# Reciprocal root of x on GpSimd, lambda product a slot later, first value projection in program order

## The chip, the cores and the metric

One core of one Trainium2 chip. The metric is the device time of one execution in microseconds (us), lower is better; the number compared is the median of several runs. The engines are named as in the profile: PE is TensorE, DVE is VectorE, ACT is ScalarE, POOL is GpSimd, and SP (SyncE) issues the weight loads. Each engine works through its own list of instructions in order; an instruction whose input isn't ready holds up everything behind it on that engine.

## What is computed

One layer of a hybrid encoder: batch 1, 256 tokens with 16 learned meta tokens ahead of them (272 in all), width 2048, in fp32.

```
def rms_norm(x, g):
    y = x * lax.rsqrt(jnp.mean(x * x, axis=-1, keepdims=True) + EPS)
    return y * g

h = concat([meta_tokens, x], axis=1)                  # 272 x 2048
u = rms_norm(h, norm_mix)
aq, ak, av, mq, mk, mv, mo, mg = split(u @ w_in)      # 1024 1024 1024 512 512 1024 1024 16
lam = exp(sum(lambda_q1 * lambda_k1)) - exp(sum(lambda_q2 * lambda_k2)) + lam_init
attn = diff_attention(rope(aq), rope(ak), av, lam)    # 8 heads, rope on a quarter of each part
ml = mlstm(silu(conv(mq, mk)), mv, gates=mg) gated by sigmoid(mo)   # 4 heads, both directions
h = h + concat([attn, ml]) @ w_out
u = rms_norm(h, norm_ffn)
h = h + (silu(u @ w_gate) * (u @ w_up)) @ w_down
out = rms_norm(h, norm_final)[16:]
```

## The kernel before

**Products in two halves.** Each fp32 product is made of three matmuls: weights are split into a high half wh, cast on ACT (line 205, with the norm's gain as scale), and a low half wl, the difference, on DVE (line 206); the input is split the same way into uh and ul. For every 128 rows k of the contraction and each of four column tiles j, PE adds wh x uh, wh x ul and wl x uh into an accumulator in PSUM (lines 251 to 253). The reciprocal root of x's norm isn't multiplied into x. It is applied to the results later: to queries and keys through the rope tables, to values as a scale.

**Pieces.** A projection of 512 columns is eight pieces of 256 rows, 512 KB each, named aq0_0, ak0_3, av_2 and so on. SP issues their loads in order; four raw buffers and four pairs of wh and wl exist. PE works on two pieces at a time, tile by tile: 48 matmuls. Four accumulators (accp) hold the four column tiles, so the next projection starts with an accumulator when the last one's has been copied out: value_copy (line 614) by ACT, into vt_q, vt_k, vt_a. Two more banks (smp) serve small products such as prs, pc, plam, pgate, psi and pct.

**The order of projections** is aq, ak, av for the first four heads (g = 0, lines 941 to 959), the same for the other four, then those of the mLSTM, the output projection and the feed-forward part. The first one, aq, is written out by hand (lines 435 to 468): x is transposed on PE, split on ACT and DVE, and its squares are summed on ACT on the way. From the sums ssx the generator x_rstd (lines 333 to 344) makes the reciprocal root of the three mean squares per partition (two blocks of tokens and the meta tokens): a first guess by integer arithmetic on the bits, three Newton steps, all on a 128x3 corner of rs3, and then rmat, the result spread over 128 columns. Its instructions come out in rstd_steps, a few with each k from 10 on. In x_broadcast (lines 346 to 354) PE transposes rmat into prs after half of the last 48 matmuls of aq, and ACT copies it to rbc; the rope tables (cst) and the gates are scaled by rbc.

**Work beside the projections** comes from generators. slot() (line 174) advances each of them by one yield with every second piece. setup() (lines 484 to 498) transposes the small vectors into cols, multiplies the lambda vectors (lprod) on DVE, and sums the products on PE (plam). gates() (lines 547 to 607) makes the mLSTM's gate terms: pgate and psi on PE, logarithms on ACT, running sums and maxima by scans on DVE (gF, gx), then gn, gem and the halves gnh and gnl, and transposes of ga and gem on PE (pct). The ropes of the four heads (rope, line 812) are issued by a hook with pieces 1 to 4 of the next projection: a shuffle and a product on DVE, a product and a sum on POOL. attention() begins with stack(h) (line 832), which splits queries and keys of a head into halves qs, ks and klow.

**What sets the order on each engine.** A scheduler puts instructions in order by a simulated time and by priorities. Where code calls pin(...), which is keep_in_program_order (line 198), the instruction stays in the order of the program text among the pinned ones. In the kernel before, all of aq is pinned, the first piece of ak, and (pins=4) the three that follow it; the splits of av, the ropes of the heads, the gate steps and attention are not.

Of the kernel before, what the change touches and what calls it, by code (L numbers as in the profile page):

```python
# [86 lines left out]
def tile_hybrid_encoder_layer(  # L87
# [42 lines left out]
    def f(ap):  # L130
        return ap.bitcast(F32)
# [201 lines left out]
    def x_rstd():  # L333
        ms, y, t, h = (rs3[:, 3 * i:3 * i + 3] for i in range(4))
        yield V.tensor_reduce(ms[:, 0:2], ssx[:, :8].rearrange("p (b c) -> p b c", c=4), AX.X, ALU.add)
        yield V.tensor_copy(ms[:, 2:3], ssx[:, 8:9])
        yield V.tensor_scalar(ms, ms, 1.0 / D, EPS, ALU.mult, ALU.add)
        yield V.tensor_scalar(y.bitcast(I32), ms.bitcast(I32), -0.5, RSQRT_MAGIC, ALU.mult, ALU.add)
        yield V.tensor_scalar(h, ms, -0.5, None, ALU.mult)
        for _ in range(3):  # L340
            yield V.tensor_tensor(t, y, y, ALU.mult)
            yield V.tensor_tensor(t, t, h, ALU.mult)
            yield V.scalar_tensor_tensor(y, t, 1.5, y, ALU.add, ALU.mult)
        yield V.tensor_copy(rmat, rs3[:, 3:6, None].to_broadcast([P, 3, P]))

# [77 lines left out]
    def rstd_steps(n):  # L423
        for _ in range(n):
            ins = next(rstd, None)
            if ins is not None:
                pin(ins)
# [10 lines left out]
    for k in range(KD - TAILK):  # L438
# [4 lines left out]
        if k >= 10:  # L443
            rstd_steps(4 if k < 13 else 16)
        order = [(j, term) for j in range(4) for term in range(3)]
# [38 lines left out]
    def setup():  # L484
# [4 lines left out]
        lprod = mp.tile([64, 2], F32, name="lprod")  # L489
        V.tensor_tensor(lprod, cols[:64, V_LAM:V_LAM + 4:2], cols[:64, V_LAM + 1:V_LAM + 4:2], ALU.mult)  # L490
        yield
        plam = sm_tile("plam")
# [54 lines left out]
    def gates():  # L547
# [15 lines left out]
        def gt(name, w=NT):  # L563
# [23 lines left out]
        yield  # L587
        V.memset(gx, 0.0)
        V.tensor_tensor_scan(gx[:32], ones[:32], ga[:32], 0.0, ALU.mult, ALU.max)
        V.tensor_tensor_scan(  # L590
            gx[32:64, NM:][:, ::-1], ones[32:64, NM:], ga[32:64, NM:][:, ::-1], 0.0, ALU.mult, ALU.max
        )
        V.tensor_scalar(gn, gx[:, NM:], -1.0, None, ALU.mult)
        V.tensor_tensor(gem, gn, gF[:, NM:], ALU.subtract)
        A.copy(gnh[:64], apart(gn))
        V.tensor_tensor(gnl[:64], apart(gn), f(gnh[:64]), ALU.subtract)
        A.activation(gem, gem, AF.Exp)
        yield
        yield
# [211 lines left out]

    def rope(ps, t0, name):
        n = NT - t0
        dst = kpool.tile([P, n], F32, tag="qk", bufs=32, name=name)
        sh = mp.tile([P, NT], F32, tag="ev", bufs=4, name=f"sh_{name}")
        swap = list(range(8, 16)) + list(range(8)) + list(range(16, 32))
        V.stream_shuffle(sh[:, :n], ps[:, :n], swap)
        V.tensor_tensor(dst, ps[:, :n], ropeC[:, t0:], ALU.mult)
        G.tensor_tensor(sh[:, :n], sh[:, :n], ropeS[:, t0:], ALU.mult)
# [9 lines left out]
    def attention(h0, nh):  # L829
        es, at, hs, on, qs, ks = {}, {}, {}, {}, {}, {}  # L830

        def stack(h):
# [4 lines left out]
            for c in range(2):  # L837
# [4 lines left out]
                A.copy(ks[h][other, c], kc)  # L842
                V.scalar_tensor_tensor(
                    qs[h][other, c, :], q[own], QK_SCALE, f(qs[h][own, c, :]), ALU.mult, ALU.subtract
                )
                V.tensor_tensor(kz[own, c], kc, f(ks[h][own, c]), ALU.subtract)

# [85 lines left out]

    def roping(vts, t0, dst, name, g):
        def hook(i):
            if 1 <= i <= 4:
                dst[4 * g + i - 1] = rope(vts[i - 1], t0, f"{name}_{4 * g + i - 1}")

        return hook

    for g in range(2):
# [13 lines left out]
        vts = value_copy(accs, f"k{g}")  # L955
        accs = in_proj(C_AV + g * N_CHUNK, 0, f"av{g}", hook=roping(vts, 0, ak, "ak", g))
        vts = value_copy(accs, f"a{g}")
# [254 lines left out]
```

## Time and profile before

| | |
|---|---|
| median of 3 runs | 1129.65 us (1129.14 to 1129.94) |
| the profiled execution | 1129.36 us, span of the trace 1127.6 us |
| PE busy | 1112.6 us, 99% |
| DVE busy | 730.7 us, 65% |
| ACT busy | 655.5 us, 58% |
| POOL busy | 246.8 us, 22% |
| read from HBM | 209.45 MB, 188 GB/s over the span |

The span runs from the first to the last instruction in the trace; the device time is 1.8 us longer. Shares are averages over the whole span. A timeline row gives the start, the duration, engine, line, operation and tiles (output <- inputs); durations of neighbours can overlap, since an instruction starts while the one before it is still writing, so the distance from start to start is the step. "idle before <- releaser" is time in which the engine waited, and who ended it.

### The profile page before, as it was taken

How to read it: one execution, taken by the hardware profiler on the slowest of the kernel's cores; microseconds unless marked ns; L12 is line 12 of the kernel's file. 1: busy time of each engine (PE TensorE's matmuls, PEld its weight loads, DVE VectorE, ACT ScalarE, POOL GpSimd, SP SyncE). 2: the span in 40 equal slices, each digit the busy share in tenths (PEclk: the TensorE clock that was granted, in tenths of full speed). 3: DMA queues.
4: the chain of work that ended last, by engine and by line, in shares of the span. 5: the costliest groups of instructions: out<-in, count | busy, mean ns of one | idle time of the engine just before them, and what ended most of it. 6: DMA issues, size and time to landing. Idle time of an engine off the chain costs nothing.

```text
span 1127.6 us, 19817 instructions
## 1 busy us (share of the span) xinstructions
PE 1112.6 (99%) x7629; PEld 1040.6 (92%) x7629; DVE 730.7 (65%) x1121; ACT 655.5 (58%) x1199; POOL 246.8 (22%) x315
## 2 busy tenths in 40 slices
PE   8999999999999999999999999999999999999996
PEld 8889999999999999999999999999999888888896
DVE  6986987988875867556556655655655645444544
ACT  6568788789875545545545555554554644444443
POOL 7330230011045933222122122122122100000000
PEclk9999999999999999999999999999999999999998
DMA  8546545554545666576576666675666766666663
GB/s 267 173 139 198 150 151 165 153 169 144 157 150 175 190 200 199 176 229 188 189 229 190 190 222 188 197 221 188 199 222 185 244 207 202 199 196 205 194 199 112
DMA packets 112255, 212.85 MB, mean 189 GB/s; under 512 B 8906, under 2 KB 9744, under 8 KB 112016
## 3 DMA queue, kind: packets, MB, share of 16 engines
q1 hardware_dynamic: 111664, 210.48, 59.9%
q8 instruction: 60, 0.98, 0.4%
q10 hardware_dynamic: 176, 1.06, 0.3%
q14 instruction: 35, 0.29, 0.1%
q0 software_dynamic: 320, 0.04, 0.0%
HBM read 209.45 MB, written 2.10 MB: 188 GB/s over the span
## 4 chain that ended last, share of the span: by engine, by line
PE 92%; DVE 3%; DMA 1%; ACT 1%; issue 1%; POOL 1%; SPq 0%; ACTq 0%; DVEq 0%; POOLq 0%
PE acc_up L248 14%; PE acc_ga L248 14%; PE acc_ga L249 7%; PE acc_up L249 7%; PE acc_dn L1108 7%; PE acc_dn L1105 7%; PE acc_dn L1109 7%; PE acc_wo L253 2%; PE acc_wo L251 2%; PE acc_wo L252 2%; PE acc_mv L252 1%; PE acc_mv L251 1%; PE acc_mv L253 1%; PE acc_mo L252 1%; PE acc_mo L251 1%; PE acc_mo L253 1%
## 5 line engine op out<-in xcount | busy, mean ns | idle before, releaser
L248 PE MATMUL acc_ga<-vhl,wh_ga 128*128 128x512 f32 x704 | 227.4, 382 | 0.0
L248 PE MATMUL acc_up<-vhl,wh_up 128*128 128x512 f32 x704 | 227.0, 382 | 0.0
L213 DVE TENSOR_TENSOR wl_dn<-raw_dn,wh_dn 128x1024 fp32r<-128x1024 f32 x88 | 108.5, 1234 | 115.5 <-ACT wh_dn L212 115.5
L249 PE MATMUL acc_ga<-vhl,wl_ga 128*128 128x256 f32 x704 | 182.1, 273 | 0.0
L249 PE MATMUL acc_up<-vhl,wl_up 128*128 128x256 f32 x704 | 181.6, 273 | 0.0
L213 DVE TENSOR_TENSOR wl_up<-raw_up,wh_up 128x1024 fp32r<-128x1024 f32 x88 | 115.6, 1343 | 79.3 <-ACT wh_up L212 79.3
L212 ACT CAST wh_dn<-raw_dn 128x1024 fp32r<-128x1024 f32 x88 | 92.3, 1050 | 125.8 <-PE acc_dn L1109 115.2
L213 DVE TENSOR_TENSOR wl_ga<-raw_ga,wh_ga 128x1024 fp32r<-128x1024 f32 x88 | 105.3, 1227 | 68.2 <-ACT wh_ga L212 68.2
L248 PEld LDWEIGHTS acc_ga<-vhl,wh_ga 128*128 128x128 f32 x704 | 130.8, 189 | 16.4
L248 PEld LDWEIGHTS acc_up<-vhl,wh_up 128*128 128x128 f32 x704 | 130.8, 189 | 16.3
L1105 PE MATMUL acc_dn<-wh_dn,ffh 128*128 128x512 f32 (+1 forms) x396 | 141.2, 357 | 0.0
L1109 PE MATMUL acc_dn<-wh_dn,ffl 128*128 128x512 f32 (+1 forms) x396 | 141.2, 357 | 0.0
L1108 PE MATMUL acc_dn<-wl_dn,ffh 128*128 128x512 f32 (+1 forms) x396 | 140.9, 356 | 0.0
L249 PEld LDWEIGHTS acc_up<-vhl,wl_up 128*128 128x128 f32 x704 | 134.1, 192 | 2.3
L249 PEld LDWEIGHTS acc_ga<-vhl,wl_ga 128*128 128x128 f32 x704 | 134.1, 192 | 2.2
L212 ACT CAST wh_ga<-raw_ga 128x1024 fp32r<-128x1024 f32 x88 | 89.3, 1050 | 68.6 <-PE acc_ga L248 31.8
L212 ACT CAST wh_up<-raw_up 128x1024 fp32r<-128x1024 f32 x88 | 89.2, 1051 | 56.7 <-PE acc_ga L248 31.3
L1109 PEld LDWEIGHTS acc_dn<-wh_dn,ffl 128*128 128x128 f32 x396 | 75.1, 190 | 8.2
L1108 PEld LDWEIGHTS acc_dn<-wl_dn,ffh 128*128 128x128 f32 x396 | 75.1, 190 | 8.1
L1105 PEld LDWEIGHTS acc_dn<-wh_dn,ffh 128*128 128x128 f32 x396 | 75.0, 190 | 8.0
L1079 POOL TENSOR_TENSOR sg<-up,sg 128x256 f32<-128x256 f32 x44 | 33.2, 756 | 173.0 <-DVE up L1053 173.0
L1066 POOL TENSOR_TENSOR s<-s,rbf 128x256 f32<-128x256 f32 x44 | 32.1, 732 | 174.9 <-DVE s L1053 174.9
(368 smaller groups left out, 2672.5 us busy)
## 6 DMA issues: line engine op xcount, KB each, us to landing
raw_ga<-in_w_gate_dram SPq DMA_DIRECT2D x88, 512.0 KB, 4.5
raw_up<-in_w_up_dram SPq DMA_DIRECT2D x88, 512.0 KB, 4.5
raw_dn<-in_w_down_dram SPq DMA_DIRECT2D x88, 512.0 KB, 4.6
raw_wo<-in_w_out_dram SPq DMA_DIRECT2D x32, 512.0 KB, 4.4
raw_ak<-in_w_in_dram SPq DMA_DIRECT2D x16, 512.0 KB, 4.1
raw_av<-in_w_in_dram SPq DMA_DIRECT2D x16, 512.0 KB, 4.6
raw_mv<-in_w_in_dram SPq DMA_DIRECT2D x16, 512.0 KB, 4.4
raw_mo<-in_w_in_dram SPq DMA_DIRECT2D x16, 512.0 KB, 3.9
```

Of the source, the lines that this page charges most:

```text
L212: pin(A.copy(wh, raw))
L213: pin(V.tensor_tensor(wl, raw, f(wh), ALU.subtract))
L248: T.matmul(pair, lhsT=qh[:, kk, sl], rhs=both(k), start=first, stop=False)
L249: T.matmul(pair[:, 1], lhsT=ql[:, kk, sl], rhs=xh(k), start=False, stop=last)
L251: T.matmul(o, lhsT=qh[:, kk, sl], rhs=xh(k), start=first, stop=False)
L252: T.matmul(o, lhsT=qh[:, kk, sl], rhs=xl(k), start=False, stop=False)
L253: T.matmul(o, lhsT=ql[:, kk, sl], rhs=xh(k), start=False, stop=last)
L1066: G.tensor_tensor(s1, s1, rbf, ALU.mult)
L1079: G.tensor_tensor(sgs[j], up, sgs[j], ALU.mult)
L1105: mm = T.matmul(o, lhsT=ffh[:, k, bsl], rhs=ph, start=(k == 0), stop=False)
L1108: T.matmul(o, lhsT=ffh[:, k, bsl], rhs=pl, start=False, stop=False)
L1109: T.matmul(o, lhsT=ffl[:, k, bsl], rhs=ph, start=False, stop=(k == KF - 1))
```

## The change

The steps of x_rstd move from DVE to POOL, all but the first sum; since POOL gets no form that adds and multiplies in one, each Newton step has four instructions in place of three. rstd_steps issues all of them at k = 10 instead of four each at 10, 11 and 12. setup() yields once more between lprod and plam. In gates() the steps from gx to gnl are pinned, with yields between them in other places. The eight splits of the first av projection are pinned (pins=8), and so are the DVE parts of the ropes of its hook and the DVE parts of stack for head 0.

```diff
--- before.py
+++ after.py
@@ -333,15 +333,16 @@
     def x_rstd():
         ms, y, t, h = (rs3[:, 3 * i:3 * i + 3] for i in range(4))
         yield V.tensor_reduce(ms[:, 0:2], ssx[:, :8].rearrange("p (b c) -> p b c", c=4), AX.X, ALU.add)
-        yield V.tensor_copy(ms[:, 2:3], ssx[:, 8:9])
-        yield V.tensor_scalar(ms, ms, 1.0 / D, EPS, ALU.mult, ALU.add)
-        yield V.tensor_scalar(y.bitcast(I32), ms.bitcast(I32), -0.5, RSQRT_MAGIC, ALU.mult, ALU.add)
-        yield V.tensor_scalar(h, ms, -0.5, None, ALU.mult)
+        yield G.tensor_copy(ms[:, 2:3], ssx[:, 8:9])
+        yield G.tensor_scalar(ms, ms, 1.0 / D, EPS, ALU.mult, ALU.add)
+        yield G.tensor_scalar(y.bitcast(I32), ms.bitcast(I32), -0.5, RSQRT_MAGIC, ALU.mult, ALU.add)
+        yield G.tensor_scalar(h, ms, -0.5, None, ALU.mult)
         for _ in range(3):
-            yield V.tensor_tensor(t, y, y, ALU.mult)
-            yield V.tensor_tensor(t, t, h, ALU.mult)
-            yield V.scalar_tensor_tensor(y, t, 1.5, y, ALU.add, ALU.mult)
-        yield V.tensor_copy(rmat, rs3[:, 3:6, None].to_broadcast([P, 3, P]))
+            yield G.tensor_tensor(t, y, y, ALU.mult)
+            yield G.tensor_tensor(t, t, h, ALU.mult)
+            yield G.tensor_scalar(t, t, 1.5, None, ALU.add)
+            yield G.tensor_tensor(y, y, t, ALU.mult)
+        yield G.tensor_copy(rmat, rs3[:, 3:6, None].to_broadcast([P, 3, P]))
 
     def x_broadcast():
         prs = sm_tile("prs")
@@ -441,7 +442,7 @@
         if 2 <= k < 10:
             x_square(k - 2)
         if k >= 10:
-            rstd_steps(4 if k < 13 else 16)
+            rstd_steps(20)
         order = [(j, term) for j in range(4) for term in range(3)]
         if k == 0:
             order.sort(key=lambda o: o[1])
@@ -489,6 +490,7 @@
         lprod = mp.tile([64, 2], F32, name="lprod")
         V.tensor_tensor(lprod, cols[:64, V_LAM:V_LAM + 4:2], cols[:64, V_LAM + 1:V_LAM + 4:2], ALU.mult)
         yield
+        yield
         plam = sm_tile("plam")
         T.matmul(plam[:, :2], lhsT=ones[:64, :P], rhs=lprod, start=True, stop=True)
         lexp = mp.tile([P, 2], F32, name="lexp")
@@ -585,17 +587,19 @@
         )
         V.tensor_tensor(ga, gi, gF, ALU.subtract)
         yield
-        V.memset(gx, 0.0)
-        V.tensor_tensor_scan(gx[:32], ones[:32], ga[:32], 0.0, ALU.mult, ALU.max)
-        V.tensor_tensor_scan(
+        pin(V.memset(gx, 0.0))
+        yield
+        pin(V.tensor_tensor_scan(gx[:32], ones[:32], ga[:32], 0.0, ALU.mult, ALU.max))
+        yield
+        pin(V.tensor_tensor_scan(
             gx[32:64, NM:][:, ::-1], ones[32:64, NM:], ga[32:64, NM:][:, ::-1], 0.0, ALU.mult, ALU.max
-        )
-        V.tensor_scalar(gn, gx[:, NM:], -1.0, None, ALU.mult)
-        V.tensor_tensor(gem, gn, gF[:, NM:], ALU.subtract)
+        ))
+        pin(V.tensor_scalar(gn, gx[:, NM:], -1.0, None, ALU.mult))
+        yield
+        pin(V.tensor_tensor(gem, gn, gF[:, NM:], ALU.subtract))
         A.copy(gnh[:64], apart(gn))
-        V.tensor_tensor(gnl[:64], apart(gn), f(gnh[:64]), ALU.subtract)
+        pin(V.tensor_tensor(gnl[:64], apart(gn), f(gnh[:64]), ALU.subtract))
         A.activation(gem, gem, AF.Exp)
-        yield
         yield
         pct = sm_tile("pct")
         T.transpose(pct[:NM, :64], ga[:, :NM], ident[:64, :64])
@@ -809,13 +813,13 @@
                 hT[j] = kpool.tile([P, SEQ], F32, tag="qk", bufs=32, name=f"hT{j}")
                 A.activation(hT[j], pht[:, :SEQ], AF.Copy, scale=cols[:, V_MLH + j:V_MLH + j + 1])
 
-    def rope(ps, t0, name):
+    def rope(ps, t0, name, pin=unpinned):
         n = NT - t0
         dst = kpool.tile([P, n], F32, tag="qk", bufs=32, name=name)
         sh = mp.tile([P, NT], F32, tag="ev", bufs=4, name=f"sh_{name}")
         swap = list(range(8, 16)) + list(range(8)) + list(range(16, 32))
-        V.stream_shuffle(sh[:, :n], ps[:, :n], swap)
-        V.tensor_tensor(dst, ps[:, :n], ropeC[:, t0:], ALU.mult)
+        pin(V.stream_shuffle(sh[:, :n], ps[:, :n], swap))
+        pin(V.tensor_tensor(dst, ps[:, :n], ropeC[:, t0:], ALU.mult))
         G.tensor_tensor(sh[:, :n], sh[:, :n], ropeS[:, t0:], ALU.mult)
         G.tensor_tensor(dst, dst, sh[:, :n], ALU.add)
         return dst
@@ -840,10 +844,11 @@
                 kc = apart(k[own])
                 A.copy(ks[h][own, c], kc)
                 A.copy(ks[h][other, c], kc)
-                V.scalar_tensor_tensor(
+                order = pin if h == 0 else unpinned
+                order(V.scalar_tensor_tensor(
                     qs[h][other, c, :], q[own], QK_SCALE, f(qs[h][own, c, :]), ALU.mult, ALU.subtract
-                )
-                V.tensor_tensor(kz[own, c], kc, f(ks[h][own, c]), ALU.subtract)
+                ))
+                order(V.tensor_tensor(kz[own, c], kc, f(ks[h][own, c]), ALU.subtract))
 
         def stats(h):
             g = h // 2
@@ -931,10 +936,10 @@
                 yield
         attending.remove(h0)
 
-    def roping(vts, t0, dst, name, g):
+    def roping(vts, t0, dst, name, g, pin=unpinned):
         def hook(i):
             if 1 <= i <= 4:
-                dst[4 * g + i - 1] = rope(vts[i - 1], t0, f"{name}_{4 * g + i - 1}")
+                dst[4 * g + i - 1] = rope(vts[i - 1], t0, f"{name}_{4 * g + i - 1}", pin)
 
         return hook
 
@@ -953,7 +958,10 @@
             C_AK + g * N_CHUNK, 0, f"ak{g}", pre=() if g else pre, pins=0 if g else 4, hook=hook
         )
         vts = value_copy(accs, f"k{g}")
-        accs = in_proj(C_AV + g * N_CHUNK, 0, f"av{g}", hook=roping(vts, 0, ak, "ak", g))
+        accs = in_proj(
+            C_AV + g * N_CHUNK, 0, f"av{g}", pins=0 if g else 8,
+            hook=roping(vts, 0, ak, "ak", g, unpinned if g else pin),
+        )
         vts = value_copy(accs, f"a{g}")
         urgent.append(value_natural(vts, lambda j, g=g: val[:, :, 4 * g + j, :], f"a{g}"))
         pending.append(attention(4 * g, 4))
```

**POOL, at the end of the projection aq.** rs is the corner with the mean squares and their roots, wgp the split gate weights, cst the rope tables, sh_aq a rope's shuffled copy. Before:

```order
L362 TENSOR_TENSOR ul<-scr,uh 128x16x8 x2
L551 TENSOR_TENSOR wgp<-wg,wgp 128x16x16
L479 TENSOR_TENSOR cst<-cst,rbc 128x272
L819 TENSOR_TENSOR sh_aq_580<-sh_aq_580,cst 128x256
L819 TENSOR_TENSOR sh_aq_586<-sh_aq_586,cst 128x256
```

and with the change:

```order
L363 TENSOR_TENSOR ul<-scr,uh 128x16x8 x2
L553 TENSOR_TENSOR wgp<-wg,wgp 128x16x16
L336 COPY rs_98<-ssx 128x1
L337 TENSOR_SCALAR rs_98<-rs_98 128x3
L338 TENSOR_SCALAR rs_98<-rs_98 128x3
L339 TENSOR_SCALAR rs_98<-rs_98 128x3
L341 TENSOR_TENSOR rs_98<-rs_98 128x3
L342 TENSOR_TENSOR rs_98<-rs_98 128x3
...
L343 TENSOR_SCALAR rs_98<-rs_98 128x3
L344 TENSOR_TENSOR rs_98<-rs_98 128x3
L345 COPY rmat<-rs_98 128x384
L480 TENSOR_TENSOR cst<-cst,rbc 128x272
```

The chain of the reciprocal root stands between wgp and the scaling of the rope table (L479 before, L480 now); the four rows from L341 to L344 come three times.

**ACT, at the seam from the projection ak to av.** ga is a gate term, wh_av_0 to 3 are the high halves of the first four pieces of av, vt_k the copies of ak's four accumulators. Before:

```order
L578 ACTIVATE ga<-ga,ones 64x272
L205 ACTIVATE wh_av_0_950<-raw_av_0_948,gm 128x512 x2
L205 ACTIVATE wh_av_1_964<-raw_av_1_962,gm 128x512 x2
L614 COPY vt_k_928<-acc_ak_0_603 128x272
L614 COPY vt_k_930<-acc_ak_1_604 128x272
L614 COPY vt_k_932<-acc_ak_2_605 128x272
L205 ACTIVATE wh_av_2_1026<-raw_av_2_1024,gm 128x512 x2
L205 ACTIVATE wh_av_3_1040<-raw_av_3_1038,gm 128x512 x2
L614 COPY vt_k_934<-acc_ak_3_606 128x272
```

and with the change:

```order
L580 ACTIVATE ga<-ga,ones 64x272
L618 COPY vt_k_931<-acc_ak_0_606 128x272
L618 COPY vt_k_933<-acc_ak_1_607 128x272
L618 COPY vt_k_935<-acc_ak_2_608 128x272
L618 COPY vt_k_937<-acc_ak_3_609 128x272
L205 ACTIVATE wh_av_0_946<-raw_av_0_944,gm 128x512 x2
L205 ACTIVATE wh_av_1_960<-raw_av_1_958,gm 128x512 x2
L205 ACTIVATE wh_av_2_1023<-raw_av_2_1021,gm 128x512 x2
```

The casts wh_av_0 and wh_av_1 stood ahead of the four copies and wh_av_2 and 3 ahead of the last; now all of them stand behind all four.

**DVE, in the projection av.** wl_av are the low halves, sh_ak and ak a rope, gx the running maximum of the gates (both scans are printed as SCALAR_TENSOR_TENSOR), gnm the tile of gn and gem. Before:

```order
L206 SCALAR_TENSOR_TENSOR wl_av_0_951<-raw_av_0_948,gm,wh_av_0_950 128x512 x2
L586 TENSOR_TENSOR ga<-gi,gF 64x272
L206 SCALAR_TENSOR_TENSOR wl_av_1_965<-raw_av_1_962,gm,wh_av_1_964 128x512 x2
L817 STREAM_SHUFFLE sh_ak_957<-vt_k_928 128x272
L818 TENSOR_TENSOR ak_956<-vt_k_928,cst 128x272
L589 SCALAR_TENSOR_TENSOR gx<-ones,ga 32x272
L590 SCALAR_TENSOR_TENSOR gx<-ones,ga 32x256
L817 STREAM_SHUFFLE sh_ak_1019<-vt_k_930 128x272
L818 TENSOR_TENSOR ak_1018<-vt_k_930,cst 128x272
L817 STREAM_SHUFFLE sh_ak_1033<-vt_k_932 128x272
L818 TENSOR_TENSOR ak_1032<-vt_k_932,cst 128x272
L593 TENSOR_SCALAR gnm<-gx 64x256
```

and with the change:

```order
L588 TENSOR_TENSOR ga<-gi,gF 64x272
L206 SCALAR_TENSOR_TENSOR wl_av_0_947<-raw_av_0_944,gm,wh_av_0_946 128x512 x2
L821 STREAM_SHUFFLE sh_ak_953<-vt_k_931 128x272
L822 TENSOR_TENSOR ak_952<-vt_k_931,cst 128x272
L206 SCALAR_TENSOR_TENSOR wl_av_1_961<-raw_av_1_958,gm,wh_av_1_960 128x512 x2
L821 STREAM_SHUFFLE sh_ak_1015<-vt_k_933 128x272
L822 TENSOR_TENSOR ak_1014<-vt_k_933,cst 128x272
L592 SCALAR_TENSOR_TENSOR gx<-ones,ga 32x272
L206 SCALAR_TENSOR_TENSOR wl_av_2_1024<-raw_av_2_1021,gm,wh_av_2_1023 128x512 x2
L821 STREAM_SHUFFLE sh_ak_1030<-vt_k_935 128x272
L822 TENSOR_TENSOR ak_1029<-vt_k_935,cst 128x272
L206 SCALAR_TENSOR_TENSOR wl_av_3_1038<-raw_av_3_1035,gm,wh_av_3_1037 128x512 x2
```

The product ga moved ahead of wl_av_0; the ropes and scans stood together ahead of wl_av_2, and now a rope stands between one piece and the next.

## Rows read from the trace of the kernel before

**Rows 1.** The page: the span, the busy times of all engines over the whole execution (us, share of the span, number of instructions), and from the list of DMA issues one load (count, KB each, median us from issue to landing).

```profile
span 1127.6 us, 19817 instructions
...
PE 1112.6 (99%) x7629; PEld 1040.6 (92%) x7629; DVE 730.7 (65%) x1121; ACT 655.5 (58%) x1199; POOL 246.8 (22%) x315
...
raw_ak<-in_w_in_dram SPq DMA_DIRECT2D x16, 512.0 KB, 4.1
```

**Rows 2.** The table by stretch (start and end in us, length, then for each engine busy us and the instructions that start there, the granted clock as a share of full speed, the DMA share and GB/s).

```profile
30.00:40.00 10.00, 9.09 (x72) 8.25 (x71) 9.76 (x31) 5.27 (x12) 3.73 (x5) 1.00 0.55 159
...
70.00:80.00 10.00, 8.99 (x67) 7.62 (x65) 9.53 (x16) 5.86 (x11) 7.14 (x5) 1.00 0.37 105
...
90.00:120.00 30.00, 30.00 (x270) 29.93 (x270) 22.75 (x49) 26.50 (x69) 2.81 (x4) 1.00 0.59 166
```

**Rows 3.** The view of the tile acc_av, the accumulators of the first value projection, from 60 to 100 us: its first matmul group (ns min/median/max, first and last start), and what PE's idle time ahead of its matmuls waited for (us, times).

```profile
L251 PE MATMUL acc_av<-uh,wh_av x64: 279/279/383, 65.2 to 91.1; 128*128 128x272 f32 x64
...
  DVE wl_av L206: 3.7, 11
```

**Rows 4.** VectorE's timeline from 27.9 to 36 us (start, duration in us, engine, line, operation, tiles, shapes, how many in a row; in brackets idle time ahead and who ended it).

```profile
27.91 0.17 DVE L338 TENSOR_SCALAR rs<-rs 128x3 int32<-128x3 int32 x1
...
29.22 1.21 DVE L206 SCALAR_TENSOR_TENSOR wl_aq<-raw_aq,gm,wh_aq 128x512 fp32r<-128x512 f32 x1 [0.20 <-ACT wh_aq L205]
...
30.43 0.15 DVE L341 TENSOR_TENSOR rs<-rs 128x3 f32<-128x3 f32 x1
30.61 0.17 DVE L342 TENSOR_TENSOR rs<-rs 128x3 f32<-128x3 f32 x1
...
30.89 0.42 DVE L395 TENSOR_TENSOR ul<-ptx,uh 128x256 fp32r<-128x256 f32 x1
31.22 0.74 DVE L206 SCALAR_TENSOR_TENSOR wl_aq<-raw_aq,gm,wh_aq 128x512 fp32r<-128x512 f32 x1
...
33.93 0.55 DVE L344 COPY rmat<-rs 128x384 f32<-128x384 f32 x1
34.42 1.41 DVE L206 SCALAR_TENSOR_TENSOR wl_ak<-raw_ak,gm,wh_ak 128x512 fp32r<-128x512 f32 x2
...
35.76 0.44 DVE L817 STREAM_SHUFFLE sh_aq<-vt_q 128x256 f32<-128x256 f32 x1
```

**Rows 5.** TensorE's timeline at the broadcast prs, at the first matmul of the next projection, and at plam; same columns.

```profile
34.66 0.39 PE L348 MATMUL prs<-ident,rmat 16*128 16x16 f32 x2
...
36.89 0.36 PE L251 MATMUL acc_ak<-uh,wh_ak 128*128 128x272 f32 x1
...
40.57 0.28 PE L252 MATMUL acc_ak<-ul,wh_ak 128*128 128x272 f32 x1
41.47 0.38 PE L493 MATMUL plam<-lprod,ones 64*128 64x2 f32 x2 [0.62 <-DVE lprod L490]
```

**Rows 6.** GpSimd's timeline from 28 to 30 us, the last instructions ahead of the ropes.

```profile
28.04 0.18 POOL L674 CAST vmeta<-ones 16x4 fp32r<-16x4 f32 x1
28.30 0.89 POOL L362 TENSOR_TENSOR ul<-scr,uh 128x128 fp32r<-128x128 f32 x2
29.15 0.73 POOL L551 TENSOR_TENSOR wgp<-wg,wgp 128x256 fp32r<-128x256 f32 x1
```

**Rows 7.** GpSimd's timeline at the ones of vml, three of four instructions of one kind at about 242 us.

```profile
241.28 0.73 POOL L623 TENSOR_SCALAR vml<-ones 128x8 fp32r<-128x8 f32 x1 [10.58 <-PE po L894]
...
241.98 0.91 POOL L623 TENSOR_SCALAR vml<-ones 128x8 fp32r<-128x8 f32 x1
...
242.90 0.23 POOL L623 TENSOR_SCALAR vml<-ones 128x8 fp32r<-128x8 f32 x1
```

**Rows 8.** VectorE's timeline at the same time.

```profile
240.50 2.07 DVE L206 SCALAR_TENSOR_TENSOR wl_mv<-raw_mv,gm,wh_mv 128x512 fp32r<-128x512 f32 x3
```

**Rows 9.** The view of groups by line, with shapes apart, for GpSimd: the group of vml (busy us, mean ns of one, idle time ahead).

```profile
L623 POOL TENSOR_SCALAR vml<-ones 128x8 fp32r<-128x8 f32 x4 | 1.8, 546 | 10.6 <-PE po L894 10.6
```

**Rows 10.** SyncE's timeline at 30.5 us, the issue of the load raw_ak of the second projection's third piece.

```profile
30.46 0.37 SPq L193 DMA_DIRECT2D raw_ak<-in_w_in_dram  x1
```

**Rows 11.** ScalarE's timeline around the seam between the projections ak and av.

```profile
60.06 2.55 ACT L205 ACTIVATE wh_av<-raw_av,gm 128x512 fp32r<-128x512 f32 x4
...
64.05 0.39 ACT L614 COPY vt_k<-acc_ak 128x272 f32<-128x272 f32 x1 [0.90 <-PE acc_ak L253]
```

**Rows 12.** VectorE's timeline over the first value projection.

```profile
60.65 0.71 DVE L582 TENSOR_TENSOR_SCAN gF<-ones,ga 32x272 f32<-32x272 f32 x1
...
62.09 1.42 DVE L206 SCALAR_TENSOR_TENSOR wl_av<-raw_av,gm,wh_av 128x512 fp32r<-128x512 f32 x2
...
65.11 0.45 DVE L817 STREAM_SHUFFLE sh_ak<-vt_k 128x272 f32<-128x272 f32 x1
...
65.81 1.28 DVE L589 TENSOR_TENSOR_SCAN gx<-ones,ga 32x272 f32<-32x272 f32 x1
...
70.64 2.06 DVE L206 SCALAR_TENSOR_TENSOR wl_av<-raw_av,gm,wh_av 128x512 fp32r<-128x512 f32 x3
72.63 0.41 DVE L594 TENSOR_TENSOR gnm<-gnm,gF 64x256 f32<-64x256 f32 x1
...
77.43 0.89 DVE L846 TENSOR_TENSOR klow<-ak,ks 64x272 fp32r<-64x272 f32 x2
78.70 3.40 DVE L206 SCALAR_TENSOR_TENSOR wl_av<-raw_av,gm,wh_av 128x512 fp32r<-128x512 f32 x5 [0.37 <-ACT wh_av L205]
```

## The prediction

> **What bounds the kernel now.** I read the page first: TensorE (PE) is busy for 1112.6 of the 1127.6 us span [rows 1]. There is little to win, and whatever PE waits for in the projections stays in the total, since every later stretch is packed as tightly as PE can run. That is seen in the table by stretch: from 90 to 120 us PE starts 270 matmuls, 90 per 10 us, but 72 from 30 to 40 and 67 from 70 to 80 [rows 2]. The change lies in those two thin stretches. Who is late there: VectorE (DVE). Over the first value projection the view of the tile acc_av counts 3.7 us in 11 waits for the low halves wl_av [rows 3]. So a part of this change is worth what it does to those moments, and a new wait of PE costs its full length.
>
> **Term A, the reciprocal root on GpSimd (POOL).** DVE loses 14 instructions of 128x3 or smaller, each a step of about 0.2 us when it depends on the one before (30.43 to 30.61), and the copy of rmat, 0.55 [rows 4]. POOL gains 17, every one waiting for the one before. What must be read is the moment rmat is ready, for PE stands at the broadcast matmul prs and cannot pass it: before, rmat ended at 34.48 [rows 4] and prs started at 34.66, 0.18 later [rows 5].
>
> When can POOL start? In its order the chain stands behind wgp, which ends at 29.15 + 0.73 = 29.9 [rows 6]; DVE had finished four of the steps by then, the fourth at 27.91 [rows 4].
>
> Price of a step. A CAST of 16x4 starts at 28.04 and the next instruction at 28.30, so 0.26 a step [rows 6]. A TENSOR_SCALAR of 128x8 that meets nothing takes 0.23 [rows 7], without a hand-over. I take 0.28. But the same TENSOR_SCALAR took 0.73 and 0.91 when DVE was running wl_mv, three two-input instructions back to back from 240.50 to 242.57 [rows 7, 8]: a small POOL instruction is held until DVE's current pass is over.
>
> Until when is DVE in such passes? With its own root steps gone it runs ul and wl of the last k, then two wl_ak: the pass of 29.22 ends at 30.4, then two ul (0.33 each, 30.89 to 31.22) and four wl (0.67 each, half of 34.42 to 35.76) [rows 4]: to 33.75. In these 3.85 us one chain step ends with each of five passes and one in each gap between them: 7 of 16. Nine are left at 0.28, 2.5, then rmat, for which I take 0.5, between the 128x8 at 0.23 [rows 7] and a TENSOR_TENSOR of 128x256 at 0.73 [rows 6]: 36.75. Add the 0.18: prs at 36.95. **A = +2.3 us.** DVE's earlier wl_aq are of no use, because PE then waits at prs instead.
>
> Here a rule that speaks against the move. The rows say 0.23 to 0.26 for a small instruction on POOL [rows 6, 7] against 0.2 on DVE [rows 4]. The Trainium skill's "GPSIMD Engine Reference", section "Engine selection", advises against elementwise work on this engine and calls two-input work about 2 times slower there. By it a step would be 0.4 (an estimate: twice DVE's 0.2), A = +3.4 and the time 1133.4, between the forecast and rival 3.
>
> Bounds of A. Above: all 17 steps at the mean of the disturbed group, 0.55 [rows 9], would end at 39.25, A = +4.8. Below: were the chain free, ScalarE (ACT) would still hold the next projection: its copies that free the PSUM banks now stand behind wh_ak_2, whose load is issued at 30.46 [rows 10] and takes 4.1 to land [rows 1]; with two casts (a quarter of 2.55 each) and a copy of 0.39 [rows 11], 34.6 + 1.3 + 0.4 is 36.3 against 36.89 when acc_ak began [rows 5], so A is not below -0.6.
>
> **Term B', lprod a slot later.** The matmul plam waited for lprod: 40.57 to 41.47 is 0.90 [rows 5] where a matmul's step is 0.11 (30 us by 270, [rows 2]). In the new order plam stands 96 places later, and lprod will be long done: **-0.8 us.** No wait takes its place at once: from the first acc_ak matmul to the first use of wl_ak_1 there are 39 matmuls, 4.3 us by that step, and of DVE's work only cols, cst, a shuffle, gda, lprod and one wl stand ahead, at most about 0.7 each by [rows 4] and mostly shorter.
>
> **Term B, the first value projection.** The pins put its eight splits in program order, and on ACT that is behind the four copies vt_k. Before, wh_av_0 and wh_av_1 were cast from 60.06 to 62.6, while PE was still on acc_ak, and PE went on without a gap at 65.2 [rows 11, 3]. Now wh_av_0 starts after vt_k_3, which needs the last acc_ak matmul. The cost: 0.3 for that matmul to end, 0.35 for the copy, 0.7 for the cast (a quarter of 2.55 with its tail), 0.1 of hand-overs [rows 11], so 1.4 after the last start instead of 0.1: PE idle for 1.3 us. DVE loses its lead as well: wl_av_0 began at 62.09, 3.1 us before PE [rows 12], now with PE.
>
> What the new order buys is that ga, gem, gnl and the klow of one head leave the stretch from wl_av_0 to wl_av_4. Before, that stretch took DVE from 62.09 to 78.70 + 0.75 = 79.45, 17.4 us, 0.4 of it idle. Taking off gem (0.41), ga and gnl (of that size, taken like it) and klow (0.9) leaves 14.9 [rows 12]. From the other side, undisturbed steps: 9 wl of 0.67, 4 ropes of 0.7 (65.11 to 65.81), 2 scans of 0.7, klow 0.9, gnm 0.3 (an estimate below gem's) make 11.4, and eight POOL instructions of the ropes hold DVE some 0.5 each (a scan took 1.28 beside them, 0.71 alone), 15.4 [rows 12]. I take 15.2. PE has 104 matmuls ahead of wl_av_4, 12.1 us. Both start at 1.4, so PE waits 15.2 - 12.1 = 3.1 us in two or three places, plus about 0.1 for each of four restarts. B = 1.3 + 3.1 + 0.4 - 3.7 = **+1.1 us.** Bounds: undisturbed ropes, 11.4, no waits: -2.4; all prices of before kept with nothing taken off: +3.
>
> The pins on qs, kz and the later gate steps move work behind PE's need of it, at nothing, covered by the rest of this projection's matmuls; without that cover they would cost their 0.4 each. Later stretches keep their work and change places by one or two rows; I set nothing, give or take 0.7.
>
> **Sum.** 2.3 - 0.8 + 1.1 = +2.6 on the profiled execution's 1129.36, or 1131.96; that execution lies 0.29 under the median of 1129.65, so I forecast **1132.3 us** for the median. About 0.2% (2.26 us) is what a measurement of this kernel can tell from no change: 1127.4 to 1131.9 is "the same".
>
> **Rivals.**
> 1. *The value projection is repaid.* If POOL's ropes do not lengthen DVE's passes, DVE reaches wl_av_4 after 11.4 us, under PE's 12.1, and the eleven waits vanish: B = 1.3 - 3.7 = -2.4 and the sum is -0.9, **1128.8**, not slower. It decides at 0.7 us of disturbance in the stretch. For it: three wl in a row ran at 0.7 each from 70.64 [rows 12]. Against it: the scan's 1.28 in the same stretch. Chance 0.12.
> 2. *The chain is not held.* If steps this small slip between DVE's passes, sixteen of 0.28, 0.5 and 0.18 from 29.9 put prs at 35.1: A = +0.4, sum +0.7, **1130.4**. Against it 0.73 and 0.91 in [rows 7]. Chance 0.14.
> 3. *The steps are dear.* At 0.55 a step, A = +4.8, sum +5.1, **1134.8**. For it a chain of 17 waits, none of which can be covered by the next instruction, and an int32 form that POOL runs nowhere before. Chance 0.14.
> That the change does not do what it says is ruled out by the order of the built program.
>
> **How the numbers follow.** The forecast has 0.57: of that 0.46 above 1131.9 and 0.11 in "the same"; rival 1 gives 0.08 same, 0.04 faster; rival 2 all same; rival 3 all slower; 0.03 is for what I don't see, spread evenly. Slower 0.61, same 0.34, faster 0.05. The forecast's own range is 1130.9 to 1134.1; with rivals 2 and 3 it becomes 1130.0 to 1135.0, leaving out rival 1 and the ends, under 0.2.
>
> **What the profile after would show.** prs starting near 37, with PE's wait put down to POOL; chain steps of 0.25 to 0.3 after 33.8 and of 0.6 to 0.9 before; no wait at plam; about 1.2 us of PE idle put down to wh_av at the first acc_av matmul; waits for wl_av_2 and wl_av_4 of 1 us or more. I am wrong if prs starts before 35.5, or if PE's waits for wl_av fall under 1.5 us.

## The result and the profile after

The changed kernel takes **1134.88 us** (median of 6 runs, 1134.15 to 1135.11) against 1129.39 us (1129.03 to 1129.94) for the kernel before on the same chip: a ratio of 1.0045, with a 95% interval of 1.0035 to 1.0055. It is slower, as was forecast, and by twice as much: 5.5 us, not 2.65. The time lies at the upper end of the range that was widened for the rivals (1130.0 to 1135.0) and above the forecast's own (1130.9 to 1134.1). The profiled execution took 1135.11 us, 5.75 more than that of before.

The page of the changed kernel shows nearly the same busy time on every engine, 14 instructions fewer on VectorE (rmat among them), 17 more on GpSimd, and a longer span [rows 1].

```profile
span 1133.3 us, 19822 instructions
...
PE 1112.7 (98%) x7629; PEld 1042.5 (92%) x7629; DVE 727.5 (64%) x1107; ACT 654.5 (58%) x1199; POOL 250.3 (22%) x332
```

**The chain on GpSimd.** GpSimd's timeline from wgp to rmat, and VectorE's last pass in that time, against [rows 4, 6]:

```profile
29.90 0.65 POOL L336 COPY rs<-ssx 128x1 f32<-128x1 f32 x1
30.64 0.20 POOL L337 TENSOR_SCALAR rs<-rs 128x3 f32<-128x3 f32 x1
...
33.55 0.20 POOL L344 TENSOR_TENSOR rs<-rs 128x3 f32<-128x3 f32 x1
33.82 0.19 POOL L341 TENSOR_TENSOR rs<-rs 128x3 f32<-128x3 f32 x1
...
36.08 0.50 POOL L345 COPY rmat<-rs 128x384 f32<-128x384 f32 x1
```

```profile
31.42 1.40 DVE L206 SCALAR_TENSOR_TENSOR wl_ak<-raw_ak,gm,wh_ak 128x512 fp32r<-128x512 f32 x2
```

The chain starts behind wgp at 29.90. VectorE's passes last until 32.8 (31.42 + 1.40), and five steps run beside them. Each ends with a pass of VectorE: four take 0.63 to 0.65, and the one of 0.20 ends at 30.84 with a pass that was nearly over. Once VectorE is idle a step is 0.26 to 0.32 from start to start, and rmat takes 0.50.

**TensorE at prs**, against [rows 5]. Timeline of the changed kernel:

```profile
36.63 0.60 PE L349 MATMUL prs<-ident,rmat 16*128 16x16 f32 x2 [3.61 <-POOL rmat L345]
...
38.39 0.42 PE L416 MATMUL acc_aq<-ul,wh_aq 128*128 128x256 f32 x1
38.61 0.42 PE L416 MATMUL acc_aq<-uh,wl_aq 128*128 128x256 f32 x1
...
40.81 0.57 PE L251 MATMUL acc_ak<-uh,wh_ak 128*128 128x272 f32 x1
```

prs starts at 36.63 instead of 34.66, 2.0 later, after 3.6 us in which TensorE had nothing to do. But the first acc_ak comes 3.9 later, at 40.81. Between the two, one matmul follows another after 0.22 us (38.39 to 38.61) and not 0.11. Why is in the table by stretch of 2 us (the granted clock is the third number from the end):

```profile
34.00:36.00 2.00, 0.00 (x0) 0.00 (x0) 0.65 (x4) 1.58 (x4) 1.42 (x8) 0.89 0.96 366
36.00:38.00 2.00, 1.37 (x6) 1.33 (x7) 0.12 (x1) 0.00 (x0) 0.52 (x2) 0.50 0.21 79
...
42.00:44.00 2.00, 2.00 (x18) 1.97 (x17) 2.00 (x5) 0.36 (x2) 1.28 (x1) 0.90 0.02 4
```

The granted clock is 0.50 of full speed, the lower of TensorE's two levels (1.2 GHz), from about 35.6 us, late in the wait (0.89 as the mean over 34 to 36), until about 42.4 (0.90 over 42 to 44). [Rows 2] had 1.00 throughout.

**plam** stands far behind pgate and waits for nothing (compare [rows 5]):

```profile
56.59 0.38 PE L495 MATMUL plam<-lprod,ones 64*128 64x2 f32 x2
```

**The first value projection**, against [rows 3, 11, 12]: ScalarE at the seam, VectorE, the tile acc_av (first and last start; then idle time, us and times), and the view of TensorE's waits from 60 to 100 us.

```profile
68.97 0.39 ACT L618 COPY vt_k<-acc_ak 128x272 f32<-128x272 f32 x1 [1.00 <-PE acc_ak L253]
69.25 5.01 ACT L205 ACTIVATE wh_av<-raw_av,gm 128x512 fp32r<-128x512 f32 x8
```

```profile
70.01 1.41 DVE L206 SCALAR_TENSOR_TENSOR wl_av<-raw_av,gm,wh_av 128x512 fp32r<-128x512 f32 x2 [4.19 <-ACT wh_av L205]
...
84.69 2.73 DVE L206 SCALAR_TENSOR_TENSOR wl_av<-raw_av,gm,wh_av 128x512 fp32r<-128x512 f32 x4
```

```profile
L251 PE MATMUL acc_av<-uh,wh_av x64: 279/279/383, 70.0 to 95.4; 128*128 128x272 f32 x64
...
  DVE wl_av L206: 5.8, 5
```

```profile
PE acc_av L253 <- DVE wl_av L206: 2.6, 2, 1.8
PE acc_av L251 <- ACT wh_av L205: 0.9, 1, 0.9
```

All eight casts of the first four pieces follow the last copy vt_k; TensorE and VectorE start together at 70.0. VectorE gets to the end of its first wl_av_4 at 84.69 + 0.75, 15.4 us later. TensorE's own waits are few and long now; the tile view's 5.8 us counts the waits of weight loads and of matmuls together, which overlap, and 2.6 is that of the matmuls alone. The same view of the kernel before, and two rows of TensorE's timeline there:

```profile
PE acc_av L253 <- DVE wl_av L206: 0.9, 3, 0.4
```

```profile
80.50 0.28 PE L252 MATMUL acc_av<-ul,wh_av 128*128 128x272 f32 x1
80.83 0.38 PE L253 MATMUL acc_av<-uh,wl_av 128*128 128x272 f32 x1
```

The view of waits misses part of what the kernel before lost here. At 80.83 a matmul starts 0.33 after the one ahead of it and not 0.11 or 0.12, while a single matmul is busy for 0.28, so hardly any idle time is left to count. Added up over the whole projection, from the first acc_av to the last, the starts that come more than 0.116 us after the one ahead lose about 3.6 us in the kernel before and 3.5 in the changed one.

**Later**, in the second av projection, TensorE waits for atm, a copy of attention weights that ScalarE makes. After, and before:

```profile
166.07 0.49 PE L897 MATMUL po<-val,atm 128*128 128x128 f32 x2 [0.84 <-ACT atm L886]
```

```profile
160.39 0.49 PE L892 MATMUL po<-val,atm 128*128 128x128 f32 x2 [0.16 <-ACT atm L881]
```

### The profile page after: what moved, and what is told of

The parts are those of the page before. It is cut to its first block, busy times and chain, and to the rows that moved or that the text cites. A ratio compares the mean times of both kernels' runs of the same rounds, so it can differ in the third digit from the quotient of the medians.

```text
span 1133.3 us, 19822 instructions
## 1 busy us (share of the span) xinstructions
PE 1112.7 (98%) x7629; PEld 1042.5 (92%) x7629; DVE 727.5 (64%) x1107; ACT 654.5 (58%) x1199; POOL 250.3 (22%) x332
## 4 chain that ended last, share of the span: by engine, by line
PE 90%; DVE 4%; DMA 1%; ACT 1%; issue 1%; POOL 1%; SPq 0%; ACTq 0%; DVEq 0%; POOLq 0%
PE acc_up L248 14%; PE acc_ga L248 14%; PE acc_ga L249 7%; PE acc_up L249 7%; PE acc_dn L1116 7%; PE acc_dn L1113 7%; PE acc_dn L1117 7%; PE acc_wo L251 2%; PE acc_wo L252 2%; PE acc_wo L253 2%; PE acc_mv L252 1%; PE acc_mv L251 1%; PE acc_mv L253 1%; PE acc_mo L252 1%; PE acc_mo L251 1%; PE acc_mo L253 1%
```

## Experiments

Theories. **1:** the wait at prs costs more than its length, because the granted clock falls in it and the work behind it runs at half speed. **2:** the clock falls for another reason and is no cost of the wait. **3:** the pins cost time at the seam and again later, in the attention of the first heads. "Before" is the kernel before, run on the same chip in the same session; ratios are to it.

### Chain back on VectorE

```diff
-        yield G.tensor_copy(ms[:, 2:3], ssx[:, 8:9])
+        yield V.tensor_copy(ms[:, 2:3], ssx[:, 8:9])
...
-            rstd_steps(20)
+            rstd_steps(4 if k < 13 else 16)
```

> The changed kernel with the reciprocal root back on DVE, everything else kept. Theory 1 (TensorE's wait of 3.6 us at prs makes the granted clock fall to half until 42.3 us, and the fall costs about 2.7 us on top of 2.0 for the later prs): prs at about 34.7 us, granted clock 1.00 from 30 to 50 us, time 1130.2 us (4.7 below the changed kernel's 1134.9). Theory 2 (the clock falls in this stretch for another reason than the wait, such as the thinner work of the projection's seam): the clock still falls, time about 1132.9.

Measured 1130.44 us, ratio 1.0008 (0.9998 to 1.0017): 4.4 below the changed kernel. The clock doesn't fall; the table by stretch:

```profile
30.00:40.00 10.00, 9.09 (x71) 8.20 (x70) 9.24 (x30) 7.34 (x15) 3.31 (x4) 1.00 0.53 159
```

TensorE in the same run, at prs and at the first matmuls of the next two projections:

```profile
34.59 0.39 PE L348 MATMUL prs<-ident,rmat 16*128 16x16 f32 x2
...
36.82 0.36 PE L251 MATMUL acc_ak<-uh,wh_ak 128*128 128x272 f32 x1
...
65.27 0.38 PE L251 MATMUL acc_av<-uh,wh_av 128*128 128x272 f32 x1 [0.88 <-ACT wh_av L205]
```

The changed kernel is 2.0 us behind this run at prs, 4.0 at the first acc_ak (40.81), 4.8 at the first acc_av (70.03), and still 4.8 at the wait for atm (166.07 against 161.24) and at the end of the span (1133.3 against 1128.5). So in these two executions the low clock added 2.7 to 2.8 us to the 2.0 of the later prs, and the rest of the kernel gave nothing back.

The interval of this run's ratio and that of the changed kernel's don't touch. So term A is 4.4 us by the medians (4.2 by the ratios), not 2.3, and theory 2's 1132.9 is out.

### Chain on GpSimd alone

The edit of x_rstd and rstd_steps, on the kernel before.

> The kernel before with the reciprocal root on GpSimd and nothing else. Theory 1: prs at about 36.6 us, the granted clock at 0.78 from 30 to 40 us as in the changed kernel, the first matmul of acc_ak at about 40.8; plam no longer waits, as lprod is done by then; 1129.4 + 4.7 - 0.8 = 1133.3 us. Theory 2: only the 2.0 of prs, without the 0.8: 1130.6.

Measured 1133.24 us, ratio 1.0033 (1.0021 to 1.0045): the time of theory 1. TensorE at prs, and the table by stretch:

```profile
37.16 0.39 PE L349 MATMUL prs<-ident,rmat 16*128 16x16 f32 x2 [3.50 <-POOL rmat L345]
```

```profile
36.00:38.00 2.00, 0.84 (x6) 0.81 (x7) 0.00 (x0) 0.00 (x0) 0.93 (x3) 0.97 0.77 280
38.00:40.00 2.00, 2.00 (x11) 2.00 (x11) 0.98 (x2) 0.69 (x2) 1.05 (x2) 0.50 0.04 15
40.00:42.00 2.00, 2.00 (x14) 2.00 (x14) 2.00 (x6) 0.44 (x2) 2.00 (x3) 0.68 0.01 4
```

Here the clock falls only when prs has begun, and is back sooner than in the changed kernel: over 30 to 40 us its mean is 0.89, not the 0.78 of the expectation. prs is 0.5 later than in the changed kernel, and the first acc_ak starts at 40.8 in both. The length of the fall goes with the time: in the three executions of 1132.1 to 1132.6 us the mean granted clock was 0.997, in the three of 1133.8 to 1134.8 it was 0.996.

### The wait filled

```diff
         prs = sm_tile("prs")
+        for _ in range(32):
+            pin(T.matmul(prs[:, 3 * P:], lhsT=ones[:, :P], rhs=ones[:, :P], start=True, stop=True))
```

> The changed kernel with 32 extra matmuls of 128x128 on TensorE, which nobody reads, just ahead of prs: TensorE has work while it waits for rmat. Theory 1: prs still at about 36.6 to 36.9, the granted clock stays at 1.00, the first matmul of acc_ak at about 38.9 instead of 40.8, time 1134.9 - 2.7 = 1132.2 us. Theory 2: clock and time as in the changed kernel, 1134.9 us.

Measured 1137.22 us: neither. I took a matmul of 128x128 for one pass; the trace shows two, and the 32 held TensorE until 40.50, long after rmat.

```profile
33.26 7.31 PE L350 MATMUL prs<-ones 128*128 128x128 f32 x64
```

Its time decides nothing, but the clock stayed at 1.00 and from prs to the first acc_ak it took 2.24 us (40.50 to 42.74), against 4.18 in the changed kernel and 2.23 in the kernel before [rows 5]. With 15:

> The changed kernel with 15 extra matmuls ahead of prs in place of 32 (each is two passes of 0.113 us, so 3.4 us, a little less than the wait). Theory 1: prs at about 36.6 to 36.9 us as in the changed kernel, granted clock 1.00 throughout, first matmul of acc_ak at about 38.9 instead of 40.8, time 1134.9 - 2.7 = 1132.2 us. Theory 2 (the fall of the clock is no cost of its own): 1134.9 us.

```profile
34.11 3.51 PE L350 MATMUL prs<-ones 128*128 128x128 f32 x30
37.76 0.39 PE L351 MATMUL prs<-ident,rmat 16*128 16x16 f32 x2
...
39.99 0.36 PE L251 MATMUL acc_ak<-uh,wh_ak 128*128 128x272 f32 x1
```

```profile
36.00:38.00 2.00, 1.86 (x17) 1.67 (x15) 0.78 (x4) 1.04 (x3) 1.31 (x6) 1.00 0.90 338
38.00:40.00 2.00, 2.00 (x20) 1.97 (x19) 0.57 (x2) 0.76 (x2) 0.71 (x1) 1.00 0.11 42
```

The clock stays at 1.00, and from prs to the first acc_ak it is 2.23. In all eight executions of the two runs with a filled wait the mean granted clock was 0.997 to 0.999, in the six of the changed kernel 0.995 or 0.996. The time is 1133.66 us, ratio 1.0038 (1.0023 to 1.0053), where 1132.2 was expected; the interval overlaps the changed kernel's, so the total does not show a gain. In the profiled execution the chain began at 30.57 instead of 29.90, beside passes of VectorE that lasted until 34.5, and prs came at 37.76, 1.1 later than in the changed kernel's. Over the stretch from prs to the first acc_av the gain is there: 31.1 us (37.76 to 68.9) against 33.4 (36.63 to 70.0), 2.3 us. Of that, 0.8 is left at the end of the span (1132.5 against 1133.3), with prs 1.1 later. That the fall of the clock has a price of its own is shown in the trace; that the total keeps it is shown by the run with the chain back on VectorE, above.

### The broadcast behind the last matmuls of aq

On the kernel before with the chain on GpSimd and lprod's yield:

```diff
-        if j == 1:
+        if j == 3:
             x_broadcast()
```

> The kernel before with the chain on GpSimd and lprod's yield, and the broadcast prs at the very end of aq, behind its last 12 matmuls: TensorE's wait begins 1.3 us later and is about 2.2 to 2.6 us long instead of 3.6. prs at about 37.0 and acc_ak right behind it. If the clock doesn't fall after this shorter wait: acc_ak at 37.6, time 1129.5 + 0.7 - 0.8 = 1129.4 us. If it falls as it did after 3.6 us, with some 3 us of work at half clock: 1130.9 us.

```profile
37.45 0.39 PE L349 MATMUL prs<-ident,rmat 16*128 16x16 f32 x2 [2.16 <-POOL rmat L345]
...
38.35 0.36 PE L251 MATMUL acc_ak<-uh,wh_ak 128*128 128x272 f32 x1
```

```profile
36.00:38.00 2.00, 0.55 (x4) 0.52 (x5) 0.78 (x4) 1.27 (x5) 1.12 (x4) 1.00 0.84 316
38.00:40.00 2.00, 2.00 (x19) 2.00 (x19) 1.37 (x7) 1.55 (x4) 0.37 (x1) 1.00 0.08 28
72.00:74.00 2.00, 1.03 (x6) 0.83 (x6) 2.00 (x5) 0.42 (x1) 2.00 (x2) 1.00 0.00 0
74.00:76.00 2.00, 1.62 (x8) 1.38 (x7) 2.00 (x5) 0.03 (x1) 2.00 (x2) 0.68 0.57 141
```

Measured 1130.94 us, ratio 1.0012 (1.0003 to 1.0021). That is the number of the second case, and it came another way: after the shorter wait (2.16 us) the clock did not fall. prs was late, at 37.45, and so the first acc_ak at 38.35. The clock fell later, at 74 us, behind waits for wl_av in which TensorE was busy for 1.03 of 2 us. So in this execution a shorter wait left the clock alone, and the projection av brought it down.

### The broadcast inside ak

x_broadcast and all that follows from rbc go into ak, behind its first 48 matmuls (from the kernel before with lprod's yield; the chain on GpSimd, then on VectorE):

```diff
-        if j == 1:
-            x_broadcast()
...
+                if i == 2:
+                    x_broadcast()
+                    V.tensor_tensor(ropeC, ropeC, rbc, ALU.mult)
+                    G.tensor_tensor(ropeS, ropeS, rbc, ALU.mult)
+                    for r in range(1, 5):
+                        ropes(r)
```

> The kernel before with the chain on GpSimd and lprod's extra yield, and with the broadcast prs and what follows from it (rope tables, ropes of the queries) moved from the tail of aq into the projection ak, after its first 48 matmuls. TensorE no longer stands at prs; VectorE has its low halves earlier by what the chain took there. If the wait at prs is all that made the move to GpSimd a loss: the first matmul of acc_ak at about 34.1 to 34.5 us against 36.9 before, no wait at plam, granted clock 1.00; 1129.4 - 2.6 - 0.8 = 1126.0 us. If the later rope tables make wl_ak_2 late by as much, 1128 us or more.

> The same with the chain on VectorE as before. It tells what the move to GpSimd is worth once nobody waits for it. VectorE's chain delays ul and wl_aq of the last rows, so TensorE loses its 1.5 us between 30 and 34 us again: 1127.4 us, 1.4 above the run with the chain on GpSimd. If VectorE has that time to spare, the two agree within 0.3.

Measured 1131.89 us (ratio 1.0022, 1.0012 to 1.0032) on GpSimd and 1133.29 (1.0036, 1.0023 to 1.0050) on VectorE. acc_ak did start at 34.21, 2.7 earlier than before, and all of it and more was lost by 90 us: the second case, and more than the waits for wl_ak alone (0.9 us). TensorE's largest group of waits in the first, from 40 to 90 us:

```profile
PE acc_av L253 <- DVE wl_av L206: 2.5, 4, 1.4
```

VectorE has the ropes of the queries later, among the splits of ak and av. Between the two runs the move to GpSimd is worth 1.4 us by the medians, as expected, and no time of one lies among those of the other (1131.35 to 1132.29, 1133.01 to 1134.35), though the intervals of the two ratios overlap: it seems to pay where nobody waits for its end. The profiled execution of the second is its slowest; there too the clock fell in the projection av (0.51 over 78 to 80 us).

### The pins

All pins and no other part of the change, on the kernel before:

> The kernel before with the pins of the first value projection, the gate steps, the ropes and head 0's split, and nothing else. The prediction's term B: 1129.4 + 1.1 = 1130.5 us. Theory 3 (what the ledger of the changed kernel shows: 1.0 at the seam, 0.1 in the projection itself, and 0.9 that comes later, in the attention of the first heads, where TensorE waits for ScalarE): 1131.4 us. The prediction's rival 1 (the projection is repaid): 1127.0 to 1128.8.

Measured 1131.82 us, ratio 1.0019 (1.0010 to 1.0029): +2.4 by the medians, +2.1 by the ratio, and theory 3 is the nearest. Where the time goes shows when the same matmuls are compared in both traces: the first and last wl matmul of the second aq projection, behind av, in the kernel before and with the pins, and TensorE at atm with the pins (160.39 in the kernel before):

```profile
L253 PE MATMUL acc_aq<-uh,wl_aq x64: 273/275/275, 92.8 to 116.6; 128*128 128x256 f32 x64
```

```profile
L253 PE MATMUL acc_aq<-uh,wl_aq x64: 272/275/276, 93.1 to 117.7; 128*128 128x256 f32 x64
```

```profile
162.39 0.49 PE L895 MATMUL po<-val,atm 128*128 128x128 f32 x2 [0.82 <-ACT atm L884]
```

The run with the pins is 1.1 us behind at 117 us and 2.0 at atm, and stays 2.0 behind until 1100 us. So the seam and the projection av together cost 1.1, and 0.9 comes later: 0.66 in the wait for atm, 0.24 at about 125 us. Then the changed kernel with only the eight casts on ScalarE set free:

```diff
     def split_scaled(wh, wl, raw, g, pin=unpinned, pina=None):
-        pin(A.activation(wh, raw, AF.Copy, scale=g))
+        (pina or pin)(A.activation(wh, raw, AF.Copy, scale=g))
```

> The changed kernel with the eight high halves of the first av projection not pinned on ScalarE (the low halves on VectorE stay pinned): wh_av_0 and wh_av_1 go ahead of the copies vt_k again. If the 1.0 us at the seam is the casts' place alone, TensorE goes on at the seam without a gap and the time is 1133.9 us. If VectorE is what bounds the projection (the rope of vt_k_0 and wl_av_0 follow in pinned order, and the waits for wl_av grow by what the seam gives back), 1134.7 us.

Measured 1132.77 us (three runs at 1132.4 to 1132.8, two at 1134.4 and 1134.6), ratio 1.0035 (1.0021 to 1.0048). By the medians that is 2.1 below the changed kernel, more than either case, but the intervals overlap. The traces tell more: the gap at the seam went, and most of the waits for wl_av went with it. In this execution prs came 0.7 later than in the changed kernel's (37.31), and the matmul at atm 0.7 earlier (165.34 against 166.07).

```profile
PE acc_av L255 <- DVE wl_av L206: 0.7, 2, 0.4
PE acc_av L253 <- ACT wh_av L205: 0.3, 1, 0.3
```

The splits unpinned on both engines, with the chain on VectorE (pins=0 for av in the run with the chain back):

> The changed kernel with the chain on VectorE and with the eight splits of the first av projection not pinned, on either engine; the gate steps, the ropes and head 0's split stay pinned. wh_av_0 and wh_av_1 stand ahead of the copies vt_k again. If pinning the splits is what made the projection dearer: no gap at the seam, waits for wl_av of about 2 us as with the casts alone set free, 1130.4 - 2.0 = 1128.4 us; lower by up to 0.7 if the longer wait for atm at 166 us in the changed kernel comes from them too. If the pinned ropes and scans are at fault, 1130.4 - 1.0 = 1129.4.

Measured **1127.93 us**, ratio 0.9986 (0.9977 to 0.9995): faster than both kernels by 7.0 and 1.7 us, and 2.5 us below the run that differs from it only in these pins (1130.44), with intervals that don't touch. ScalarE and VectorE at the seam, and TensorE's waits from 60 to 90 us:

```profile
59.31 2.55 ACT L205 ACTIVATE wh_av<-raw_av,gm 128x512 fp32r<-128x512 f32 x4
```

```profile
61.34 1.42 DVE L206 SCALAR_TENSOR_TENSOR wl_av<-raw_av,gm,wh_av 128x512 fp32r<-128x512 f32 x2
```

```profile
PE acc_av L253 <- DVE wl_av L206: 0.6, 1, 0.6
```

wh_av and wl_av have their lead again [rows 11, 12], and the later ropes and scans still alternate with the pieces as pinned. Of the 1.7 us below the kernel before, 0.8 is what lprod's yield brings by itself (the last run below); that the rest is a gain is not shown, as the intervals of these two runs overlap. The wait for atm stayed; it was long in every run so far with the pins and short in every one without them. Head 0's pins taken off as well:

```diff
-                order = pin if h == 0 else unpinned
+                order = unpinned
```

> As the run with the av splits set free, and head 0's split (qs and klow of the first head on VectorE) not pinned either; the gate steps and the ropes stay pinned. The wait for atm in the second av projection, at about 160 us, was 0.38 to 0.40 us in every run without these pins and 0.92 to 1.06 in every run with them. If head 0's pins cause it: 0.4 there and 1127.3 us (0.6 under the 1127.9 of that run). If the pinned ropes or gate steps do: 1.0 there and 1127.9 us.

TensorE at atm with these pins and without:

```profile
159.05 0.38 PE L896 MATMUL po<-val,atm 128*128 128x128 f32 x1 [0.74 <-ACT atm L885]
```

```profile
159.40 0.38 PE L896 MATMUL po<-val,atm 128*128 128x128 f32 x1 [0.19 <-ACT atm L885]
```

Head 0's pins cause the longer wait for atm. But the time is 1128.49 us, ratio 0.9989 (0.9980 to 0.9998), not 1127.3: TensorE's waits for wl_av went from 0.6 to 1.1 us. Between these two runs no difference is shown.

### The yield alone

> The kernel before with the extra yield between lprod and plam and nothing else. The prediction's term: plam's wait of 0.8 us goes and no other comes in its place, 1129.5 - 0.8 = 1128.7 us. By the difference of the two runs that have the pins without and with this yield (1131.82 and 1130.44): 1128.1 us. If the time comes back as another wait in the same projection: 1129.5.

Measured 1128.78 us, ratio 0.9994 (0.9985 to 1.0003): 0.8 below before in the medians, the size that was forecast and not the 1.4 that the difference of two other runs had; the interval still reaches no change.

## Why the prediction was right, and where it was wrong

**Term A was mis-sized: +2.3 forecast, 4.4 measured** (changed kernel against the run with the chain back on VectorE). The price of its steps held: a chain step waits for VectorE's pass (0.63 to 0.65), a free one is 0.28 on average (not the 0.4 of the rule against the move), rmat is 0.50, and prs started at 36.63 against 36.95. That this came out so near is in part luck: VectorE's passes ended at 32.8 and not at 33.75, and one step ended with each pass, five in all and not seven, and the two errors nearly cancel. The sentence that failed is the one that priced a wait of TensorE at its full length and no more. The clock came back only after 42 us: from prs to the first acc_ak it took 4.2 us, and 2.2 where the wait was filled. In the traces the later prs costs 2.0 us and the low clock behind it 2.7 to 2.8.

**Rivals.** Rival 1 is out, since the waits for wl_av did not vanish. Rival 2 is out, since the steps were held. Rival 3 named 1134.8 and the time came there, but not by its mechanism: the steps were not dear. The time lies in the range only because that rival had widened it, so that part is luck. The clock was no rival at all, and should have been one, since no wait of TensorE in the rows of before was nearly as long as the one that term A made.

**Term B' was right:** no wait at plam, none in its place, -0.8 by the medians.

**Term B was right in its own stretch: +1.1 forecast, 1.1 in the traces** of the pins alone, by the end of the next projection. Its parts came out too: the seam (1.3 forecast, 0.9 to 1.0 measured), VectorE's stretch (15.2 forecast, 15.4), the later waits (3.1 + 0.4 forecast, 3.5) and what was taken off for the kernel before (3.7 forecast, 3.6).

**Later stretches were mis-sized.** They were set at nothing, give or take 0.7, and in the same traces they cost 0.9: the pins as a whole come to 2.0 there, and to +2.1 to +2.4 in the times. 0.66 us is the longer wait for atm (0.82 idle against 0.16), which head 0's pins cause, and which comes 80 us behind them; the cause of the 0.24 at about 125 us stays open.

That VectorE's lead is lost was seen, and that it needn't be was not: with the eight splits free and ropes, scans and head 0 pinned as before, the time falls by 2.5 us and below both kernels. That the casts on ScalarE alone would do it is likely by the traces and not shown by the times.

## What to carry to other kernels

Price a wait of TensorE by its length and by the clock behind it: look whether waits of that length in the same trace leave the granted clock at 1.00, and if none is as long, give the fall a case of its own. Before moving a chain of small steps to another engine, look who stands at its end and what the two engines hold each other up with. Before pinning an order, look which engine's lead hides a seam, since the pins can take that lead away. To see where two kernels part, compare the starts of the same matmul in both traces; a view of waits misses starts that are only a little late.

## What was not expected of the hardware

After waits of 3.5 and 3.6 us the granted clock fell to 0.50, in one run during the wait and in the other only after work had begun again; after 2.2 us it stayed at 1.00. In another it fell at 74 us, after 2 us in which TensorE was busy for 1.03. With matmuls in the wait that nobody reads it stayed at 1.00. The Trainium skill's "TensorE: Matmul & The Clock Gate", section "Part 1: The HAM clock gate (the "warmup" mystery)", says that the array gets half of its clock pulses when it has been idle and all of them again once it has been busy, and that the moment differs from run to run; the traces agree, with 0.50 and 1.00. The page bears on this change and was not weighed in the prediction. A matmul of 128x128 in fp32 shows in the trace as two of 0.11 us (32 of them took 7.2 us). What remains open: why the moment of the fall, and with it the price, differs from one execution to the next.
